# Output projection of a hybrid decoder layer: halves of 512 columns in four PSUM banks, where there were quarters of 256

## The chip, the cores and the metric

The kernel runs on one core of one Trainium2 chip. The metric is the device time of one execution in microseconds (us); the times before are the median of three runs and one profiled execution.

## The reference

The layer normalises 2048 positions of 1024 channels, projects them for three groups of heads, concatenates the groups' outputs (384 + 384 + 256 columns), maps them through one matrix and normalises the sum with the residual:

```python
hn = rmsnorm(x, norm_g)
a_in, a_gate, c_in, c_b, c_c, c_gate, q, q_gate = split(hn @ w_in)
y_ssm  = s5_group(a_in, ..., w_glu, b_glu) * silu(a_gate)      # 384 columns
y_conv = short_conv(c_in, c_b, c_c) * silu(c_gate)             # 384 columns
y_mem  = memory_cross_attention(q, rmsnorm(mem)) * silu(q_gate) # 256 columns
h = x + concat(y_ssm, y_conv, y_mem) @ w_out                   # w_out is 1024 x 1024
out = rmsnorm(h, final_norm_g)
```

The change is in the last two lines alone.

## The kernel before

The sequence is worked on in four quarters q = 0 to 3 of 512 positions. Every product of two float32 matrices is made of three matmuls on numbers that are split into a high and a low part (`mm3`: high by high at L81, high by low at L82, low by high at L83). `split` makes the parts: ScalarE (ACT) copies the high part (a CAST at L86), and then VectorE (DVE) or GpSimd (POOL) subtracts it for the low part (a TENSOR_TENSOR at L77). `wtile` loads a weight tile through SyncE's queue (SP) into a staging buffer and splits it.

The output projection of one quarter multiplies the 8 row tiles of y (three of the state-space group, `yssm`; three of the convolution, `yconv`; two of the attention, `ymem`; 128 rows each) by `w_out`. `outproj` goes over four quarters of 256 output columns (n_). For each it holds two PSUM banks, named po with the quarter, n_ and b: each bank holds two of the four blocks i of 128 positions, side by side. Two weight tiles of 512 rows by 256 columns (kh = 0 and 1) feed it, and for each tile and block `omm` issues 12 matmuls of 256 columns. One projection is 384 matmuls. VectorE then adds each bank to the residual h (`h<-po`, 128x512); that add is what returns the bank. After the last column, ScalarE squares and sums h (L101), a row of small operations on VectorE and GpSimd makes the scale, and four products of 1024 columns at L916 finish the rows.

The four projections run at four places of the program. In the code they are:

```python
    interleave(outproj(1), prep(2), 0.3, 2)     # L1019
    interleave(outproj(0), prep(3), 0.3, 2)     # L1022
    interleave(outproj(3), glu(2), 1.0)         # L1025
    outproj_last(2)                             # L1026
```

I call them projections one to four in this order. `interleave` puts steps of a second task between the steps of the projection: `prep` loads x for the next quarter (`xq`), normalises it (a chain of small operations q22v, q22r, q22a, q22o and a product at L602) and transposes it through TensorE (`trq`, L144) into `hn`; `glu` multiplies the state-space output by `w_glu` (tiles `wg`, banks `psg`, 27 matmuls of 512 columns) and makes the gate products `gt` and `ua`, whose split is `yssm`. `outproj_last` keeps all eight weight tiles in buffers that are free by then (`wyc`, `wym`, `wtb`, `hy` and so on) and finishes blocks 0 and 1 first, then block 2, then block 3.

A scheduler fixes the order of instructions on each engine before the kernel is run, and each engine runs its queue in order: an instruction that waits holds back all that stand behind it on its engine. PSUM has eight banks: three for all projections (`ps_mm`), two for transposes, one for the attention's output (`ps_po`), two for the state-space group (`ps_ss`; `psg` is there). Split weight tiles have three buffers, their staging two.

Of the kernel before, what the change touches and what calls it, by code (L numbers as in the profile page):

```python
# [28 lines left out]
QL = SEQ // NQ  # L29
# [16 lines left out]
def hymba_layer_kernel(  # L46
# [7 lines left out]
    V, S, G, T = nc.vector, nc.scalar, nc.gpsimd, nc.tensor  # L54
# [5 lines left out]
    kvp = ctx.enter_context(tc.tile_pool(name="kvp", bufs=1))  # L60
# [39 lines left out]
    def sumsq(xt, ss, junk):  # L100
        S.activation(junk, xt, AF.Square, accum_out=ss)  # L101
# [7 lines left out]
    fg_b = const.tile([P, DM], F32, name="fg_b")  # L109
# [513 lines left out]
    yv, Y = {}, {}  # L623
# [81 lines left out]
    vd = kvp.tile([P, 2, 2, HEADS, P], F32R, tag="vd", name="vd")  # L705
# [136 lines left out]
        yield  # L842


    yk = [("ssm", 0), ("ssm", 1), ("ssm", 2), ("conv", 0), ("conv", 1), ("mem", 0), ("mem", 1), ("conv", 2)]
    rows = [0, 1, 2, 3, 4, 6, 7, 5]

    def fetch_y(q):

# [13 lines left out]
                t = Y[q]["conv" if z + k < 3 else "mem"][:, :, (z + k) % 3]  # L863
                split(t[:, 0], t[:, 1], st[:, k], V if k else G)

    def omm(q, ps, i, kh, w, first):

        o_ = slice(i * P, (i + 1) * P)
        for k in range(4):
            nm, kk = yk[4 * kh + k]  # L870
            kr = rows[4 * kh + k] - 4 * kh
            mm3(ps, Y[q][nm][:, 0, kk, o_], Y[q][nm][:, 1, kk, o_], w[:, 0, kr, :], w[:, 1, kr, :],
                first and k == 0, kh == 1 and k == 3, skip_group_check=True)

    def residual(q, last=False):

# [9 lines left out]
                nc.sync.dma_start(h[z][u * NCH:(u + 1) * NCH], xq[q, u][:, 2 * z:2 * z + 2])  # L886
        return h

    def wout(q, n_, kh, dst=None, st="w", e=G):
        src = w_out[0, kh * 512:(kh + 1) * 512, n_ * 256:(n_ + 1) * 256]  # L890
        return wtile(src, 512, 256, f"wo{q}{n_}{kh}", e, dst, st)

    def outproj(q):
        h = residual(q)
        for n_ in range(4):
            ns = slice(n_ * 256, (n_ + 1) * 256)
            pss = [ps_mm.tile([P, 2, 256], F32, tag="mm", name=f"po{q}{n_}{b}") for b in range(2)]
            for kh in range(2):
                w = wout(q, n_, kh)
                for i in range(4):  # L900
                    omm(q, pss[i // 2][:, i % 2, :], i, kh, w, kh == 0 and i % 2 == 0)
                    yield
            for b in range(2):
                hb = h[b][:, :, ns]
                tt(hb, pss[b], hb, ALU.add)
        jk = tmp.tile([P, QL], F32, tag="ci", name=f"junk{q}")
        ss = sml.tile([P, 2, 4], F32, tag="ssf", name=f"ssf{q}")
        for i in range(4):
            for z in range(2):
                sumsq(h[i // 2][:, i % 2, z * QL:(z + 1) * QL], ss[:, z, i:i + 1], jk)  # L910
        tt(ss[:, 0], ss[:, 0], ss[:, 1], ALU.add)
        ss = ss[:, 0]
        r = row_rstd(ss, 4, "rf", f"f{q}")
        for i in range(4):
            hi_ = h[i // 2][:, i % 2]
            V.scalar_tensor_tensor(hi_, hi_, r[:, i:i + 1], fg_b, ALU.mult, ALU.mult)  # L916
            for u in range(2):
                nc.sync.dma_start(oq[q, u, :, i], hi_[u * NCH:(u + 1) * NCH])
        yield

    def outproj_last(q):

        h, hb = residual(q, True)
        for u in range(2):
            nc.sync.dma_start(hb[u * NCH:(u + 1) * NCH], xq[q, u][:, 2:4])
        hg = late["big"].tile([P, 2, DM], F32, tag="big1", name="hg")

        def wv_(t):
            return t[:, :2 * 4 * 256].rearrange("p (z k n) -> p z k n", z=2, k=4)

        dsts = [None, None, None, Y[q]["rest"].rearrange("p z a (b n) -> p z (a b) n", b=2)]
        dsts.append(wv_(kvp.tile([P, 2 * 4 * 256], F32R, tag="vd", name="wvd")))
        dsts.append(wv_(stab.tile([P, GB * TW], F32, tag="tb", name="wtb").bitcast(F32R)))
        dsts.append(wv_(late["yc"].tile([P, 2 * 3 * QL], F32R, tag="yc", name="wyc")))
        dsts.append(wv_(late["ym"].tile([P, 2 * 2 * QL], F32R, tag="ym", name="wym")))
        ws = [[wout(q, n_, kh, dsts[2 * n_ + kh], "wx"[kh], V if kh else G) for kh in range(2)] for n_ in range(4)]
        ss, jk = (sml.tile([P, 4, 4], F32, tag=t_, bufs=1, name=t_) for t_ in ("ssl", "ssk"))

        def rstd(i, nss):
            V.tensor_reduce(jk[:, i, 0:1], ss[:, i, 0:nss], AX.X, ALU.add)  # L940
            return row_rstd(jk[:, i, 0:1], 1, f"rl{i}", f"fl{i}")

        def store(i, src):
            for u in range(2):
                nc.sync.dma_start(oq[q, u, :, i], src[u * NCH:(u + 1) * NCH])

        junk = [tmp.tile([P, QL], F32, tag=t_, name="junk" + t_) for t_ in ("ci", "u")]
        for n_ in range(4):
            ns = slice(n_ * 256, (n_ + 1) * 256)
            ps = ps_mm.tile([P, 2, 256], F32, tag="mm", name=f"po{q}{n_}")  # L950
            for kh in range(2):
                for i in range(2):
                    omm(q, ps[:, i, :], i, kh, ws[n_][kh], kh == 0 and i == 0)
            for i in range(2):
                tt(h[i][:, ns], ps[:, i], h[i][:, ns], ALU.add)
                sumsq(h[i][:, ns], ss[:, i, n_:n_ + 1], junk[0][:, 0:256])
        for i in range(2):
            V.scalar_tensor_tensor(h[i], h[i], rstd(i, 4), fg_b, ALU.mult, ALU.mult)
            store(i, h[i])
        for i in range(2, 4):  # L960
            parts = [(0, 1), (2, 3)] if i == 2 else [(0, 1), (2,), (3,)]
            for b, ns_ in enumerate(parts):
                ns = slice(ns_[0] * 256, ns_[-1] * 256 + 256)
                ps = ps_mm.tile([P, 2, 256], F32, tag="mm", name=f"po{q}{i}_{b}")
                for a, n_ in enumerate(ns_):
                    for kh in range(2):
                        omm(q, ps[:, a, :], i, kh, ws[n_][kh], kh == 0 and a == 0)
                pv = ps.rearrange("p a n -> p (a n)")[:, :256 * len(ns_)]
                tt(h[i][:, ns], pv, h[i][:, ns], ALU.add)
                sumsq(h[i][:, ns], ss[:, i, b:b + 1], junk[1][:, :256 * len(ns_)])  # L970
                tt(hg[:, i - 2, ns], h[i][:, ns], fg_b[:, ns], ALU.mult)
            r = rstd(i, len(parts))
            V.tensor_scalar(h[i][:, :QL], hg[:, i - 2, :QL], r, None, ALU.mult)
            S.activation(h[i][:, QL:], hg[:, i - 2, QL:], AF.Copy, scale=r)  # L974
            store(i, h[i])
# [48 lines left out]
    fetch_y(2)  # L1024
    interleave(outproj(3), glu(2), 1.0)  # L1025
    outproj_last(2)  # L1026


# [27 lines left out]
```

## Time and profile before

| what | value |
| --- | --- |
| median of 3 runs | 902.94 us (900.92 to 909.04) |
| profiled execution | 904.45 us |
| its span (first to last instruction) | 902.5 us |
| mean granted clock of TensorE in the span | 0.975 |
| TensorE (PE) busy | 843.1 us, 93% |
| VectorE (DVE) busy | 613.7 us, 68% |
| ScalarE (ACT) busy | 367.0 us, 41% |
| GpSimd (POOL) busy | 301.7 us, 33% |

A row of a timeline gives the start of an instruction in us, its length, engine, line, operation, the tiles it writes and reads, its shape and how many such follow each other; in brackets stands how long the engine was idle just before it and what released it. Matmuls overlap, so that the pace of a run of them is the distance between starts, not the length of one. "Clock" is the share of TensorE's full clock that was granted: 1.00 is 2.4 GHz and 0.50 is 1.2 GHz.

### The profile page before, as it was taken

The numbers are of one execution on the slowest core, as the hardware profiler recorded it, in microseconds if no ns is written. First come the engines' busy times: TensorE is split into PE (matmuls) and PEld (weight loads), VectorE is DVE, ScalarE is ACT, GpSimd is POOL, SyncE is SP. The second block draws the span as 40 slices with busy tenths as digits, with TensorE's granted clock in tenths as the row PEclk, the third lists the DMA queues.
The fourth block names the chain that finished last, engine by engine and source line by source line (L and its number), as shares of the span: only waits on it lengthen the run. The fifth ranks groups of instructions, "written<-read, shape, count | busy, mean of one in ns | idle before, by whom it ended". The sixth has DMA issues, their size and how long they took to land. (4 is left out here: it accounts for less than half of the span.)

```text
span 902.5 us, 13173 instructions
## 1 busy us (share of the span) xinstructions
PE 843.1 (93%) x4876; PEld 723.7 (80%) x4876; DVE 613.7 (68%) x1244; ACT 367.0 (41%) x706; POOL 301.7 (33%) x157
## 2 busy tenths in 40 slices
PE   2998999889998998999999899999999998989996
PEld 2985777778877877899888688899878876879996
DVE  6898899583998896936434664344399996865353
ACT  5343433545343434433444533335233344444511
POOL 2000001154222344444545434334443343455400
PEclk9999899999997999999999999999999999999999
DMA  9553649966464534454575632656757744493362
GB/s 205 161 150 103 189 131 269 267 187 201 125 179 130 156 93 119 108 152 141 159 239 150 160 114 84 161 165 186 214 156 207 211 128 125 117 222 112 125 177 57
DMA packets 180647, 142.97 MB, mean 158 GB/s; under 512 B 41192, under 2 KB 164584, under 8 KB 180584
## 3 DMA queue, kind: packets, MB, share of 16 engines
q1 hardware_dynamic: 180584, 142.14, 56.4%
q8 instruction: 38, 0.62, 0.3%
q14 instruction: 25, 0.20, 0.1%
HBM read 113.80 MB, written 26.74 MB: 156 GB/s over the span
## 5 line engine op out<-in xcount | busy, mean ns | idle before, releaser
L77 POOL TENSOR_TENSOR wo<-wo_st,wo 128x1024 fp32r<-128x1024 f32 x26 | 63.8, 2454 | 70.6 <-ACT wo L86 59.2
L77 DVE TENSOR_TENSOR h<-po,h 128x512 f32<-128x512 f32 (+1 forms) x37 | 22.2, 615 | 43.5 <-PE po L83 34.5
L81 PE MATMUL po<-wo,yssm 128*128 128x256 f32 x168 | 48.5, 289 | 1.8 <-ACT yssm L86 1.8
L83 PE MATMUL po<-wo,yssm 128*128 128x256 f32 x168 | 48.2, 287 | 0.0
L82 PE MATMUL po<-wo,yssm 128*128 128x256 f32 x168 | 47.8, 285 | 0.0
L780 ACT ACTIVATE pe<-sps,nm 128x256 f32<-128x256 f32 x64 | 29.5, 472 | 39.4 <-DVE nm L778 35.1
L81 PE MATMUL psai<-hn,wai 128*128 128x512 f32 (+1 forms) x120 | 42.7, 362 | 2.8 <-ACT hn L86 2.1
L82 PE MATMUL psai<-hn,wai 128*128 128x512 f32 (+1 forms) x120 | 42.5, 356 | 0.3 <-DVE hn L77 0.2
L83 PE MATMUL psai<-hn,wai 128*128 128x512 f32 (+1 forms) x120 | 42.0, 353 | 0.0
L81 PE MATMUL pscg<-hn,wcg 128*128 128x512 f32 x96 | 39.8, 415 | 2.2 <-ACT wcg L86 2.2
L86 ACT CAST wo<-wo_st 128x1024 fp32r<-128x1024 f32 x27 | 28.2, 1044 | 33.3 <-PE po L83 16.2
L81 PE MATMUL po<-wo,yconv 128*128 128x256 f32 x144 | 40.7, 283 | 0.0
L83 PE MATMUL po<-wo,yconv 128*128 128x256 f32 x144 | 40.3, 280 | 0.0
L82 PE MATMUL po<-wo,yconv 128*128 128x256 f32 x144 | 40.1, 279 | 0.0
L83 PE MATMUL pscg<-hn,wcg 128*128 128x512 f32 x96 | 39.1, 407 | 0.5 <-DVE wcg L77 0.5
L81 PE MATMUL psag<-hn,wag 128*128 128x512 f32 x96 | 39.5, 411 | 0.0
L82 PE MATMUL pscg<-hn,wcg 128*128 128x512 f32 x96 | 39.0, 407 | 0.0
L77 POOL TENSOR_TENSOR wcb<-wcb_st,wcb 128x1024 fp32r<-128x1024 f32 x9 | 22.9, 2550 | 47.9 <-ACT wcb L86 47.9
L83 PE MATMUL psag<-hn,wag 128*128 128x512 f32 x96 | 38.5, 401 | 0.0
L82 PE MATMUL psag<-hn,wag 128*128 128x512 f32 x96 | 38.4, 400 | 0.0
L81 PE MATMUL pscb<-hn,wcb 128*128 128x512 f32 x96 | 38.3, 399 | 0.0
L81 PE MATMUL psci<-hn,wci 128*128 128x512 f32 x96 | 38.3, 399 | 0.0
(710 smaller groups left out, 2903.5 us busy)
## 6 DMA issues: line engine op xcount, KB each, us to landing
wo_st<-in_w_out_dram SPq DMA_DIRECT2D x32, 512.0 KB, 3.8
tb<-t_dram SPq DMA_DIRECT2D x16, 960.0 KB, 5.5
out_dram<-h SPq DMA_DIRECT2D x32, 256.0 KB, 3.4
h<-in_x_dram SPq DMA_DIRECT2D x14, 512.0 KB, 7.4
wai_st<-in_w_in_dram SPq DMA_DIRECT2D x12, 512.0 KB, 4.3
wag_st<-in_w_in_dram SPq DMA_DIRECT2D x12, 512.0 KB, 4.3
wci_st<-in_w_in_dram SPq DMA_DIRECT2D x12, 512.0 KB, 4.2
wcc_st<-in_w_in_dram SPq DMA_DIRECT2D x12, 512.0 KB, 4.1
```

Of the source, the lines that this page charges most:

```text
L77: e.tensor_tensor(o, a, b, op)
L81: T.matmul(ps, lh, rh, start=first, stop=False, **kw)
L82: T.matmul(ps, lh, rl, start=False, stop=False, **kw)
L83: T.matmul(ps, ll, rh, start=False, stop=last, **kw)
L86: S.copy(hi, src)
L780: S.activation(pe[:, a, h], sps[h][:, a], AF.Exp, bias=nm_[:, a, h:h + 1], accum_out=sm[:, a, h:h + 1])
```

## The change

The projection goes over two halves of 512 columns. Each of the four blocks i has a bank of its own: three banks of `ps_mm` and the one of `ps_po`. A weight tile is now 256 rows by 512 columns, that is two row tiles of y (a pair kp), and holds as many elements as before; the pairs are taken in the order 0, 1, 3, 2. A call of `omm` issues 6 matmuls of 512 columns. The list `yk` has the row tiles in plain order, so the table `rows` goes. `outproj_last` does the same for its blocks 0 and 1, takes block 2 in two parts of 512 columns and block 3 in parts of 512, 256 and 256; the sums of squares of blocks 0 and 1 have two pieces in place of four.

```diff
-    yk = [("ssm", 0), ("ssm", 1), ("ssm", 2), ("conv", 0), ("conv", 1), ("mem", 0), ("mem", 1), ("conv", 2)]
-    rows = [0, 1, 2, 3, 4, 6, 7, 5]
+    yk = [("ssm", 0), ("ssm", 1), ("ssm", 2), ("conv", 0), ("conv", 1), ("conv", 2), ("mem", 0), ("mem", 1)]
+    pairs = (0, 1, 3, 2)
...
-        for k in range(4):
-            nm, kk = yk[4 * kh + k]
-            kr = rows[4 * kh + k] - 4 * kh
-            mm3(ps, Y[q][nm][:, 0, kk, o_], Y[q][nm][:, 1, kk, o_], w[:, 0, kr, :], w[:, 1, kr, :],
-                first and k == 0, kh == 1 and k == 3, skip_group_check=True)
+        for k in range(2):
+            nm, kk = yk[2 * kp + k]
+            mm3(ps, Y[q][nm][:, 0, kk, o_], Y[q][nm][:, 1, kk, o_], w[:, 0, k, cs], w[:, 1, k, cs],
+                kp == pairs[0] and k == 0, kp == pairs[-1] and k == 1)
...
-        src = w_out[0, kh * 512:(kh + 1) * 512, n_ * 256:(n_ + 1) * 256]
+        src = w_out[0, kp * 256:(kp + 1) * 256, nh * 512:(nh + 1) * 512]
...
-        for n_ in range(4):
-            ns = slice(n_ * 256, (n_ + 1) * 256)
-            pss = [ps_mm.tile([P, 2, 256], F32, tag="mm", name=f"po{q}{n_}{b}") for b in range(2)]
-            for kh in range(2):
-                w = wout(q, n_, kh)
+        for nh in range(2):
+            ns = slice(nh * 512, (nh + 1) * 512)
+            pss = [ps_mm.tile([P, 512], F32, tag="mm", name=f"po{q}{nh}{b}") for b in range(3)]
+            pss.append(ps_po.tile([P, QL], F32, tag="po", name=f"po{q}{nh}3"))
+            for kp in pairs:
+                w = wout(q, nh, kp)
                 for i in range(4):
-                    omm(q, pss[i // 2][:, i % 2, :], i, kh, w, kh == 0 and i % 2 == 0)
+                    omm(q, pss[i], i, kp, w)
                     yield
-            for b in range(2):
-                hb = h[b][:, :, ns]
-                tt(hb, pss[b], hb, ALU.add)
+            for i in range(4):
+                hb = h[i // 2][:, i % 2, ns]
+                tt(hb, pss[i], hb, ALU.add)
...
-        for n_ in range(4):
-            ns = slice(n_ * 256, (n_ + 1) * 256)
-            ps = ps_mm.tile([P, 2, 256], F32, tag="mm", name=f"po{q}{n_}")
-            for kh in range(2):
+        for nh in range(2):
+            ns = slice(nh * 512, (nh + 1) * 512)
+            pss = [ps_mm.tile([P, 512], F32, tag="mm", name=f"po{q}{nh}{i}") for i in range(2)]
+            for kp in pairs:
                 for i in range(2):
-                    omm(q, ps[:, i, :], i, kh, ws[n_][kh], kh == 0 and i == 0)
+                    omm(q, pss[i], i, kp, ws[nh][kp])
```

The four projections have 1536 matmuls of 256 columns before; with the change they have 744 of 512 and 48 of 256. Everything outside the projections keeps its order, except a few neighbouring loads on SyncE's queue. Three places move within the engines' queues; names end in a running number.

TensorE at the start of projection one, before: banks po100 and po101 on the first weight tile wo100, then the transposes of `prep`; `yssm1` in the rows after the transposes is the third row tile of the state-space group, `yssm1` ahead of them the first two.

```order
L81 MATMUL po101_3667<-wo100_3670,yssm1_3351 128x256
L82 MATMUL po101_3667<-wo100_3670,yssm1_3351 128x256
L83 MATMUL po101_3667<-wo100_3670,yssm1_3351 128x256
L144 MATMUL trq20_0_3770<-ident_99,xq20_3751 128x128 x4
L144 MATMUL trq20_1_3822<-ident_99,xq20_3751 128x128
L81 MATMUL po100_3666<-wo100_3670,yssm1_3351 128x256
L82 MATMUL po100_3666<-wo100_3670,yssm1_3351 128x256
```

The same place with the change, where the third row tile comes with the second weight tile, wo101:

```order
L83 MATMUL po101_3667<-wo100_3672,yssm1_3351 128x512
L81 MATMUL po103_3669<-wo100_3672,yssm1_3351 128x512
L82 MATMUL po103_3669<-wo100_3672,yssm1_3351 128x512
L83 MATMUL po103_3669<-wo100_3672,yssm1_3351 128x512
L81 MATMUL po100_3666<-wo101_3701,yssm1_3351 128x512
L82 MATMUL po100_3666<-wo101_3701,yssm1_3351 128x512
L81 MATMUL po101_3667<-wo101_3701,yssm1_3351 128x512
L83 MATMUL po100_3666<-wo101_3701,yssm1_3351 128x512
```

Ahead of the first matmul on the third row tile there stood 12 matmuls of 256 columns and 5 transposes; now 18 of 512 columns stand there, and the transposes come later.

TensorE in projection three, around the first matmul of `glu` (bank psg20, weight tile wg20), before:

```order
L83 MATMUL po301_7331<-wo301_7426,ymem3_6906 128x256
L81 MATMUL po310_7527<-wo310_7531,yssm3_6918 128x256
L81 MATMUL po300_7330<-wo301_7426,ymem3_6906 128x256
L82 MATMUL po300_7330<-wo301_7426,ymem3_6906 128x256
L81 MATMUL po301_7331<-wo301_7426,ymem3_6906 128x256
L82 MATMUL po301_7331<-wo301_7426,ymem3_6906 128x256
L81 MATMUL psg20_7408<-yssm2_7349,wg20_7405 128x512
L82 MATMUL psg20_7408<-yssm2_7349,wg20_7405 128x512
```

And with the change:

```order
L81 MATMUL po303_6949<-wo301_7020,yssm3_6534 128x512
L82 MATMUL po303_6949<-wo301_7020,yssm3_6534 128x512
L83 MATMUL po303_6949<-wo301_7020,yssm3_6534 128x512
L81 MATMUL psg20_7002<-yssm2_6961,wg20_6999 128x512
L82 MATMUL psg20_7002<-yssm2_6961,wg20_6999 128x512
L81 MATMUL po303_6949<-wo301_7020,yconv3_6122 128x512
L82 MATMUL po303_6949<-wo301_7020,yconv3_6122 128x512
L83 MATMUL psg20_7002<-yssm2_6961,wg20_6999 128x512
```

Ahead of the first psg20 matmul stood 65 matmuls of 256 columns of the projection; now 45 of 512 stand there.

VectorE in projection one, where `prep` normalises its third block (q22, xq22) and TensorE goes from the first columns to the next, before:

```order
L77 TENSOR_TENSOR q22a_4006<-q22r_4005 128x1
L77 TENSOR_TENSOR q22a_4006<-q22a_4006,q22v_4004 128x1
L96 TENSOR_SCALAR q22a_4006<-q22a_4006 128x1
L77 TENSOR_TENSOR q22o_4007<-q22r_4005,q22a_4006 128x1
L602 SCALAR_TENSOR_TENSOR xq22_3996<-xq22_3996,q22o_4007,ng_b_106 128x1024
L77 TENSOR_TENSOR hn2_3750<-trq21_0_3901,hn2_3750 128x4x128
L77 TENSOR_TENSOR h10_3660<-po110_3803,h10_3660 128x2x256
L77 TENSOR_TENSOR h11_3661<-po111_3804,h11_3661 128x2x256
```

And with the change, where these are the adds at the end of the first half, which return the four banks to the second half:

```order
L77 TENSOR_TENSOR q22a_3894<-q22r_3893 128x1
L77 TENSOR_TENSOR h10_3660<-po100_3666,h10_3660 128x512
L77 TENSOR_TENSOR q22a_3894<-q22a_3894,q22v_3892 128x1
L96 TENSOR_SCALAR q22a_3894<-q22a_3894 128x1
L77 TENSOR_TENSOR q22o_3895<-q22r_3893,q22a_3894 128x1
L77 TENSOR_TENSOR hn2_3716<-trq21_0_3821,hn2_3716 128x4x128
L602 SCALAR_TENSOR_TENSOR xq22_3884<-xq22_3884,q22o_3895,ng_b_106 128x1024
L77 TENSOR_TENSOR h10_3660<-po101_3667,h10_3660 128x512
L77 TENSOR_TENSOR h11_3661<-po102_3668,h11_3661 128x512
L77 TENSOR_TENSOR h11_3661<-po103_3669,h11_3661 128x512
```

The add of the first bank stands inside the chain, the adds of the other three behind the product at L602. In projection four the adds of the first half (po200, po201) stand on VectorE behind the four products of L916, where the add of the first bank of 256 columns stood ahead of them.

## Rows read from the trace of the kernel before

**Rows 1.** The page: busy time, share of the span, instructions; granted clock in 40 slices.
```profile
PE 843.1 (93%) x4876; PEld 723.7 (80%) x4876; DVE 613.7 (68%) x1244; ACT 367.0 (41%) x706; POOL 301.7 (33%) x157
PEclk9999899999997999999999999999999999999999
```

**Rows 2.** Windows, one per projection: us, PE busy (count), clock, DMA share, GB/s.
```profile
381.01:433.26 52.25, 50.43 (x417) 0.97 0.54 146
578.25:626.52 48.27, 48.27 (x417) 1.00 0.69 196
791.31:848.37 57.06, 53.07 (x412) 0.97 0.64 171
848.37:893.84 45.47, 45.47 (x386) 1.00 0.42 117
```

**Rows 3.** Timeline of PE: first matmuls that bound runs without a wait.
```profile
433.26 0.40 PE L81 MATMUL psai<-hn,wai 128*128 128x512 f32 x1
...
449.61 0.39 PE L81 MATMUL psq<-hn,wq 128*128 128x512 f32 x1
...
826.13 0.28 PE L81 MATMUL po<-wo,yssm 128*128 128x256 f32 x1
```

**Rows 4.** Windows of PE after waits and, fourth row, in a run.
```profile
386.56:389.97 3.41, 3.41 (x18) 0.50 0.83 174
389.97:393.38 3.41, 3.41 (x31) 1.00 0.46 153
802.50:806.49 3.99, 3.90 (x10) 0.57 1.04 186
788.53:791.31 2.78, 2.78 (x13) 1.00 0.43 109
...
354.20:362.00 7.80, 6.18 (x28) 1.00 0.48 135
675.40:679.00 3.60, 1.71 (x12) 1.00 0.50 148
```

**Rows 5.** Timelines of PE, ACT and DVE at the start of projection one.
```profile
384.96 0.39 PE L81 MATMUL po<-wo,yssm 128*128 128x256 f32 x1 [1.81 <-ACT yssm L86]
...
384.29 0.62 ACT L86 CAST yssm<-ua 128x512 fp32r<-128x512 f32 x1 [0.76 <-DVE ua L838]
...
384.94 0.94 DVE L77 TENSOR_TENSOR yssm<-ua,yssm 128x512 fp32r<-128x512 f32 x1 [0.74 <-ACT yssm L86]
```

**Rows 6.** Timelines of PE, ACT and DVE in projection three, around `glu`'s tiles.
```profile
802.49 0.50 PE L81 MATMUL psg<-yssm,wg 128*128 128x512 f32 x1 [3.40 <-ACT wg L86]
...
810.64 0.50 PE L81 MATMUL psg<-yssm,wg 128*128 128x512 f32 x1 [0.50 <-ACT wg L86]
...
801.92 0.51 ACT L86 CAST wg<-wg_st 128x384 fp32r<-128x384 f32 x1 [4.44 <-DMA wg_st<-in_w_glu_dram]
...
810.08 0.51 ACT L86 CAST wg<-wg_st 128x384 fp32r<-128x384 f32 x1 [2.64 <-DMA wg_st<-in_w_glu_dram]
...
802.47 0.88 DVE L77 TENSOR_TENSOR wg<-wg_st,wg 128x384 fp32r<-128x384 f32 x1 [0.67 <-ACT wg L86]
```

**Rows 7.** Timelines in the middle of projection one: VectorE, GpSimd, SyncE.
```profile
406.06 2.40 DVE L77 TENSOR_TENSOR q22a<-q22r 128x1 f32<-128x1 f32 x1 [0.66 <-POOL q22r L77]
...
409.06 1.28 DVE L602 SCALAR_TENSOR_TENSOR xq<-xq,q22o,ng_b 128x1024 f32<-128x1024 f32 x1
...
410.86 1.28 DVE L77 TENSOR_TENSOR h<-po,h 128x512 f32<-128x512 f32 x2
...
406.03 2.41 POOL L77 TENSOR_TENSOR wo<-wo_st,wo 128x1024 fp32r<-128x1024 f32 x1
...
398.70 1.14 SPq L572 DMA_DIRECT2D xq<-in_x_dram  x2
```

**Rows 8.** Timeline of VectorE in projection four.
```profile
859.46 4.87 DVE L916 SCALAR_TENSOR_TENSOR h<-h,f3o,fg_b 128x1024 f32<-128x1024 f32 x4
864.25 0.75 DVE L77 TENSOR_TENSOR h<-po,h 128x256 f32<-128x256 f32 x2
```

More of the change, by code (lines that the diff above doesn't have):

```diff
@@ L864, in fetch_y, with omm @@
                 split(t[:, 0], t[:, 1], st[:, k], V if k else G)
-    def omm(q, ps, i, kh, w, first):
+    def omm(q, ps, i, kp, w, cs=slice(0, 512)):
         o_ = slice(i * P, (i + 1) * P)
-        for k in range(4):
-            nm, kk = yk[4 * kh + k]
-            kr = rows[4 * kh + k] - 4 * kh
-            mm3(ps, Y[q][nm][:, 0, kk, o_], Y[q][nm][:, 1, kk, o_], w[:, 0, kr, :], w[:, 1, kr, :],
-                first and k == 0, kh == 1 and k == 3, skip_group_check=True)
+        for k in range(2):
+            nm, kk = yk[2 * kp + k]
+            mm3(ps, Y[q][nm][:, 0, kk, o_], Y[q][nm][:, 1, kk, o_], w[:, 0, k, cs], w[:, 1, k, cs],
+                kp == pairs[0] and k == 0, kp == pairs[-1] and k == 1)
     def residual(q, last=False):
@@ L887, in residual, with wout @@
         return h
-    def wout(q, n_, kh, dst=None, st="w", e=G):
-        src = w_out[0, kh * 512:(kh + 1) * 512, n_ * 256:(n_ + 1) * 256]
-        return wtile(src, 512, 256, f"wo{q}{n_}{kh}", e, dst, st)
+    def wout(q, nh, kp, dst=None, st="w", e=G):
+        src = w_out[0, kp * 256:(kp + 1) * 256, nh * 512:(nh + 1) * 512]
+        return wtile(src, 256, 512, f"wo{q}{nh}{kp}", e, dst, st)
     def outproj(q):
         h = residual(q)
-        for n_ in range(4):
-            ns = slice(n_ * 256, (n_ + 1) * 256)
-            pss = [ps_mm.tile([P, 2, 256], F32, tag="mm", name=f"po{q}{n_}{b}") for b in range(2)]
-            for kh in range(2):
-                w = wout(q, n_, kh)
+        for nh in range(2):
[4 more added lines that the diff above has]
+                w = wout(q, nh, kp)
                 for i in range(4):
-                    omm(q, pss[i // 2][:, i % 2, :], i, kh, w, kh == 0 and i % 2 == 0)
+                    omm(q, pss[i], i, kp, w)
                     yield
-            for b in range(2):
-                hb = h[b][:, :, ns]
-                tt(hb, pss[b], hb, ALU.add)
+            for i in range(4):
+                hb = h[i // 2][:, i % 2, ns]
+                tt(hb, pss[i], hb, ALU.add)
         jk = tmp.tile([P, QL], F32, tag="ci", name=f"junk{q}")
@@ L928, in wv_ @@
         def wv_(t):
-            return t[:, :2 * 4 * 256].rearrange("p (z k n) -> p z k n", z=2, k=4)
-        dsts = [None, None, None, Y[q]["rest"].rearrange("p z a (b n) -> p z (a b) n", b=2)]
-        dsts.append(wv_(kvp.tile([P, 2 * 4 * 256], F32R, tag="vd", name="wvd")))
+            return t[:, :2 * 2 * 512].rearrange("p (z k n) -> p z k n", z=2, k=2)
+        dsts = [None, None, None, Y[q]["rest"]]
+        dsts.append(wv_(kvp.tile([P, 2 * 2 * 512], F32R, tag="vd", name="wvd")))
         dsts.append(wv_(stab.tile([P, GB * TW], F32, tag="tb", name="wtb").bitcast(F32R)))
@@ L935, in outproj_last @@
         dsts.append(wv_(late["ym"].tile([P, 2 * 2 * QL], F32R, tag="ym", name="wym")))
-        ws = [[wout(q, n_, kh, dsts[2 * n_ + kh], "wx"[kh], V if kh else G) for kh in range(2)] for n_ in range(4)]
+        ws = [{kp: wout(q, nh, kp, dsts[4 * nh + a], "wx"[a % 2], V if a % 2 else G) for a, kp in enumerate(pairs)}
+              for nh in range(2)]
         ss, jk = (sml.tile([P, 4, 4], F32, tag=t_, bufs=1, name=t_) for t_ in ("ssl", "ssk"))
@@ L954, in outproj_last @@
             for i in range(2):
-                tt(h[i][:, ns], ps[:, i], h[i][:, ns], ALU.add)
-                sumsq(h[i][:, ns], ss[:, i, n_:n_ + 1], junk[0][:, 0:256])
+                tt(h[i][:, ns], pss[i], h[i][:, ns], ALU.add)
+                sumsq(h[i][:, ns], ss[:, i, nh:nh + 1], junk[0])
         for i in range(2):
-            V.scalar_tensor_tensor(h[i], h[i], rstd(i, 4), fg_b, ALU.mult, ALU.mult)
+            V.scalar_tensor_tensor(h[i], h[i], rstd(i, 2), fg_b, ALU.mult, ALU.mult)
@@ L959, in outproj_last @@
             store(i, h[i])
         for i in range(2, 4):
[L961 to L970, printed above, removed]
+            parts = [(0, 512), (512, 1024)] if i == 2 else [(0, 512), (512, 768), (768, 1024)]
@@ L971, in outproj_last @@
+            for b, (c0, c1) in enumerate(parts):
+                ns = slice(c0, c1)
+                ps = ps_mm.tile([P, 512], F32, tag="mm", name=f"po{q}{i}_{b}")[:, :c1 - c0]
+                for kp in pairs:
+                    omm(q, ps, i, kp, ws[c0 // 512][kp], slice(c0 % 512, c0 % 512 + c1 - c0))
+                tt(h[i][:, ns], ps, h[i][:, ns], ALU.add)
+                sumsq(h[i][:, ns], ss[:, i, b:b + 1], junk[1][:, :c1 - c0])
                 tt(hg[:, i - 2, ns], h[i][:, ns], fg_b[:, ns], ALU.mult)
```

## The prediction

> **What bounds the kernel now.** I read the page's busy shares first. TensorE is busy 93% of the span, VectorE 68%, and nearly all slices have TensorE at full clock [rows 1]: so what counts is the number and pace of matmuls, and the few places where TensorE waits. Then I cut the span into the four projections, the only stages that the change touches [rows 2]. Projections one and two have the same instructions, 384 matmuls of 256 columns and 32 transposes, but one takes 52.25 us and two 48.27; two has no idle time, one has. Three is 57.06 us with 4.0 idle; four has none. Together they are 203 us. Last I read the waits inside them in the timelines. Wherever the waits are gone, TensorE itself is the bound, and only a faster pace helps.
>
> **The pace.** 72 matmuls of 512 columns run from 433.26 to 449.61 without a wait: 227.1 ns each. The second half of projection three, from 826.13 to 848.37, is 192 matmuls of 256 columns and nothing else: 115.8 ns each, 231.7 for a pair [rows 2, 3]. A pair that becomes one matmul saves 4.6 ns, times 192 pairs a projection, 0.88 us; for projections one to three 2.6 us. Projection four takes 45.47 us for 384, 236.8 ns a pair [rows 2]; at 227.1 each of its 168 pairs saves 9.7 ns, 1.6 us (24 pairs stay as they are). Together -4.3 us. The other bound: the 12 matmuls of 512 columns just ahead of projection three took 2.78 us, 231.7 ns each [rows 4]; at that pace projections one to three gain nothing and four gains 168 x 5.1 ns, 0.9 us. I take 227.1, since it is a run of 72 in a row with the same operand types, and keep -0.9 for the range.
>
> The Trainium skill, "TensorE: Matmul & The Clock Gate", section "Back-to-back issue gap", gives the isolated gap of a matmul at full clock as its columns by 2.4 plus 2.5 ns: 109.2 for 256 columns, 215.8 for 512. By that a pair would save 2.5 ns, 1.9 us over 744 pairs in place of 4.3, and the whole sum would come to 893.6. The trace disagrees on both sizes: 115.8 and 227.1.
>
> **The wait at the start of projection one.** TensorE idles 1.81 us until ScalarE's CAST of the third `yssm` row tile, and then runs at half clock from 386.56 to 389.97: 18 instructions there, 31 in the next 3.41 us [rows 4, 5]. Against projection two the whole costs 52.25 - 48.27 = 4.0 us: 1.8 waiting, 3.41 x 0.5 = 1.7 of clock, 0.5 of small gaps. With the change 18 matmuls of 512 columns stand ahead of the third tile, so TensorE comes there at 381.01 + 18 x 0.2271 = 385.10. The high part is done at 384.29 + 0.62 = 384.91, the low part at 384.94 + 0.94 = 385.88; the first matmul that needs the low one comes three later, at 385.78 [rows 5]. A wait of 0.1 is left: -3.9 us. What comes next is weight tile wo101, split before the projection begins. If the 0.1 grows and the clock falls anyway, 1.7 of the 3.9 stays.
>
> **The waits in projection three.** Its first half, 791.31 to 826.13, takes 34.82 us; 192 matmuls at 115.8 ns are 22.24 and 27 of `glu` at 227.1 are 6.13, so 6.4 us are lost [rows 2, 3]: waits of 3.40 and 0.50 for `wg` tiles [rows 6], 3.99 x 0.43 = 1.7 us of clock behind the first [rows 4], and 0.8 of small gaps. With the change 45 matmuls of 512 columns (in place of 65 of 256) stand ahead of psg20: TensorE comes at 791.31 + 45 x 0.2271 = 801.53. The tile's load is not moved, and ScalarE's CAST ends at 801.92 + 0.51 = 802.43 [rows 6]. A wait of 0.9 is left. The low part, at 803.35 [rows 6], is wanted four matmuls later, at 803.34: nothing. psg21 has 81 matmuls ahead of it: 791.31 + 0.9 + 81 x 0.2271 = 810.6, its CAST ends at 810.59 [rows 6]: nothing. Does a wait of 0.9 bring the clock down? After 1.81 it fell; but two windows with 1.6 and 1.9 us of idle time in them kept 1.00 [rows 4], so I take that it stays up. -5.5 us; the bounds are -3.0 (1.7 of clock and 0.8 of gaps stay) and -6.4.
>
> **What the change adds: banks that come back in fours.** Before, a projection held two of three banks, and the next columns began in the third. Now all four are held; at the end of a half TensorE needs the first one back at once. Its add (0.64 us, [rows 7]) can run once the last pair is through with block 0, 18 matmuls or 4.1 us before the half ends. But in projections one and two it stands in VectorE's queue behind q22a, and the three other adds behind the product at L602. That chain starts with the load of xq22, which went out at 398.70, after the last transpose of xq20 [rows 7]. In the new order that transpose has 54 matmuls and 7 transposes of about 0.12 us ahead of it: 381.01 + 12.3 + 0.8 = 394.1, 4.5 us earlier. If the chain moves by that, q22a starts at 401.6 and the first add is done at 402.4 to 404.6; TensorE ends the half at 381.01 + 96 x 0.2271 + 16 x 0.12 = 404.7. L602 then ends at 405.8, and the three adds by 408.4, while the other banks are wanted from 407.2 on, some 1.4 us apart. So it just fits. But q22a, one column wide, took 2.40 us while GpSimd ran a subtraction of 2.41 us from 406.03 on [rows 7]; where they meet depends on the new times. Behind a late add in VectorE's queue stand the copies `hn<-trq`, which return transpose banks, and TensorE waits for those too. I charge 0.5 us in each of the two projections; bounds 0 and 2.4, the row of q22a. In projection three VectorE is nearly idle at the half's end: 0.
>
> In projection four po211 needs the bank of po200, whose add stands behind the four products of L916. These end at 859.46 + 4.87 = 864.33, 16.0 us after the projection's start, the add 0.7 later [rows 8]; TensorE comes there after 72 matmuls, 16.35 us. Its wait is 0.35 if nothing ahead of the products is later than before; the sums of squares and GpSimd's step are. I charge 1.0; bounds 0 and 3.4 (the longest wait in these rows [rows 6]).
>
> Loads and splits have the same number, size and staging as before, and each weight tile feeds 24 matmuls of 512 columns in place of 48 of 256, so nothing there. The two sums of squares fewer a block run on ScalarE, beside TensorE. The end after the last matmul is unchanged.
>
> **The sum.** -4.3 - 3.9 - 5.5 + 1.0 + 1.0 = -11.7 us. From the profiled 904.45 that gives 892.75; the median of the runs lies 1.5 lower, so 902.94 - 11.7 = 891.2 us.
>
> **The rivals.** First, the clock still falls behind the shorter waits in projections one and three: 1.7 of the one and 2.5 of the other stay. For it: half clock follows both waits there now [rows 4]. Against: two idle times of that size that cost no clock [rows 4]. -11.7 + 4.2 = -7.5, 895.4 us; if projection four waits its 3.4 as well, 897.8.
>
> Second, the change doesn't give the pace that it is made for: 512 columns at 231.7 ns. -0.9 for -4.3 gives -8.3, 894.6 us. For it: one such run [rows 4]. Against: the run of 72.
>
> Third, the other side: the banks come back late at each boundary. If xq22's chain is not earlier than before, the first add of projection one ends at 406.06 + 2.40 + 0.64 = 409.1, while TensorE wants the bank at 404.7: 4.4 us, and half clock behind it another 1.7, 6.1 in place of the 0.5 charged, in projections one and two; in projection four 3.4 + 1.7 = 5.1 in place of 1.0. That is +15.3 on -11.7: 906.5 us, slower than before. It decides from (11.7 + 2.0) / 3 = 4.6 us a boundary on, clock included. Against it: the load of xq22 waits for a transpose that does come earlier. The Trainium skill has a rule for this: the same page, section "A second HAM failure mode: psum-queue depth-cycling", tells of a kernel with matmuls of 512 columns that cycled through PSUM banks, idled shortly between groups and lost its clock over and over. The trace of before doesn't show it: there the next columns always found a spare bank.
>
> Fourth, better: nothing of the added waits comes, and projection three loses all its 6.4: -14.6, 888.3 us.
>
> **How the numbers follow.** Forecast 0.53, clock 0.22, pace 0.12, late banks 0.08, better 0.05. The forecast's own spread, with 0 to 2.4 twice and 0 to 3.4 for the costs, is 888 to 896. The range of 885 to 901 takes in all cases but the third, and half of what lies between it and the first. 1% is 9.0 us, about what a measurement of this kernel can tell from no change; it puts the border at 893.9. Below it lie most of the forecast (0.46), the better case (0.05) and a part of the two middle ones (0.06): 0.57 faster. Slower by over 1% would be 912, which needs the third case and a wait in projection three as well: 0.04. The rest, 0.39, is the same.
>
> **What would show it.** Right: starts of matmuls 227 ns apart in the projections; projections one and two 47 to 48 us, three 50 to 51, four 45; no wait over 0.5 us for `yssm` at 385 and one near 0.9 before psg20; adds of the first bank done before the second half's first matmul. Wrong: slices of TensorE at half clock at the middles of the projections, with `h<-po` as what ended the wait; pairs at 232 ns; a load of xq22 that goes out no earlier.

## The result, and the profile after

The changed kernel takes 896.89 us (median of 8 runs, 895.24 to 899.31) where the kernel before took 903.98 (8 runs beside them): a ratio of 0.9921, 95% interval 0.9898 to 0.9944. That is 7.1 us less, by 0.8%: the whole interval lies below 1, but the gain is within the 1% that the prediction calls the same; 11.7 us had been forecast. The page of its profile, busy time and granted clock [rows 1]:

```profile
span 895.1 us, 11674 instructions
PE 837.5 (94%) x4132; PEld 686.3 (77%) x4132; DVE 613.9 (69%) x1240; ACT 365.1 (41%) x698; POOL 300.7 (34%) x157
PEclk9999899989997999999999999999999999999998
```

The windows of its four projections [rows 2], then one behind the wait at psg20 [rows 4], then the last 96 matmuls of projection three (stretch, us, PE busy with count, clock, DMA share, GB/s):

```profile
382.10:431.43 49.33, 48.39 (x226) 1.00 0.56 152
575.57:623.70 48.13, 48.05 (x226) 1.00 0.68 198
786.46:840.83 54.37, 52.15 (x221) 0.97 0.63 178
840.83:886.44 45.61, 44.28 (x217) 1.00 0.43 119
800.49:803.90 3.41, 3.41 (x9) 0.50 1.06 304
818.91:840.83 21.92, 21.92 (x98) 1.00 0.52 162
```

Projection one is 2.9 us shorter, two 0.1 and three 2.7, and four is 0.1 longer: 5.6 us less in all. The rest of the span's 7.4 lies in stretches that the change doesn't touch: 1.1 us more ahead of projection one, 0.8 less between one and two, 2.0 less between two and three. The wait at the start of one is gone, with its half clock. Four waits of TensorE are left, here from its timeline with what ended them:

```profile
407.26 0.47 PE L81 MATMUL po<-wo,yssm 128*128 128x512 f32 x1 [0.92 <-DVE q22a L77]
797.87 0.50 PE L81 MATMUL psg<-yssm,wg 128*128 128x512 f32 x1 [1.02 <-ACT wg L86]
800.27 0.64 PE L83 MATMUL psg<-yssm,wg 128*128 128x512 f32 x1 [1.21 <-DVE wg L77]
858.73 0.50 PE L81 MATMUL po<-wvd,yssm 128*128 128x512 f32 x1 [1.33 <-DVE h L77]
```

And VectorE at these places: the chain of q22 with the first bank's add [rows 7], the weight tile of the gate behind the subtraction for `yconv` [rows 6], and the add of po200 behind the four products [rows 8]:

```profile
404.14 2.38 DVE L77 TENSOR_TENSOR q22a<-q22r 128x1 f32<-128x1 f32 x1 [0.66 <-POOL q22r L77]
406.44 0.68 DVE L77 TENSOR_TENSOR h<-po,h 128x512 f32<-128x512 f32 x1
...
795.81 2.86 DVE L77 TENSOR_TENSOR yconv<-uc,yconv 128x512 fp32r<-128x512 f32 x1
798.60 1.62 DVE L77 TENSOR_TENSOR wg<-wg_st,wg 128x384 fp32r<-128x384 f32 x1
...
853.20 4.88 DVE L916 SCALAR_TENSOR_TENSOR h<-h,f3o,fg_b 128x1024 f32<-128x1024 f32 x4
857.99 0.68 DVE L77 TENSOR_TENSOR h<-po,h 128x512 f32<-128x512 f32 x1
```

Each of the four waits ends with VectorE or, for the high part, with ScalarE's CAST: at these places, 4.5 of the 197.4 us, the path has gone from TensorE's own pace to what the other two give back. (The profile puts the first wait down to the small q22a behind the add; e_ss below shows that it is the bank's.)

My theory after this one execution: the gain is the pace, the start of one and a part of three; what is missing is that three keeps two waits and one piece of half clock, and that the banks cost 0.9 and 1.3 us. The rivals: that the pace brought less than all this, or nothing; and that the missing part is chance in stretches elsewhere.

### The profile page after: what moved, and what is told of

Read it like the earlier page. It is cut to its first block, busy times and chain, and to the rows that moved or that the text cites. A ratio compares the mean times of both kernels' runs of the same rounds, so it can differ in the third digit from the quotient of the medians.

```text
span 895.1 us, 11674 instructions
## 1 busy us (share of the span) xinstructions
PE 837.5 (94%) x4132; PEld 686.3 (77%) x4132; DVE 613.9 (69%) x1240; ACT 365.1 (41%) x698; POOL 300.7 (34%) x157
## 5 line engine op out<-in xcount | busy, mean ns | idle before, releaser
L81 PE MATMUL psai<-hn,wai 128*128 128x512 f32 (+1 forms) x120 | 43.4, 368 | 3.8 <-ACT hn L86 2.8
L82 PE MATMUL psai<-hn,wai 128*128 128x512 f32 (+1 forms) x120 | 43.2, 362 | 0.3 <-DVE hn L77 0.2
L83 PE MATMUL psai<-hn,wai 128*128 128x512 f32 (+1 forms) x120 | 42.7, 359 | 0.0
L81 PE MATMUL pscb<-hn,wcb 128*128 128x512 f32 x96 | 38.3, 399 | 0.0
L81 PE MATMUL psci<-hn,wci 128*128 128x512 f32 x96 | 38.2, 398 | 0.0
L81 PE MATMUL pscc<-hn,wcc 128*128 128x512 f32 x96 | 38.2, 398 | 0.0
L83 PE MATMUL pscb<-hn,wcb 128*128 128x512 f32 x96 | 37.7, 393 | 0.0
L82 PE MATMUL pscc<-hn,wcc 128*128 128x512 f32 x96 | 37.7, 392 | 0.0
L83 PE MATMUL psci<-hn,wci 128*128 128x512 f32 x96 | 37.7, 392 | 0.0
L82 PE MATMUL pscb<-hn,wcb 128*128 128x512 f32 x96 | 37.6, 392 | 0.0
L83 PE MATMUL pscc<-hn,wcc 128*128 128x512 f32 x96 | 37.6, 392 | 0.0
L82 PE MATMUL psci<-hn,wci 128*128 128x512 f32 x96 | 37.6, 392 | 0.0
```

## The experiments

All ratios are to the kernel before, run beside them on the same chip. It took 905.1 to 906.0 us there, so that the changed kernel, at 0.9921, stands for 897.9 to 898.9, 1 to 2 us above the 896.9 that the expectations start from. The lengths in us of the projections, and of the stretch from the end of two to the start of three, are from one profiled execution each:

| run | one | two | two to three | three | four | ratio (95%) |
| --- | --- | --- | --- | --- | --- | --- |
| before | 52.25 | 48.27 | 164.79 | 57.06 | 45.47 | |
| changed | 49.33 | 48.13 | 162.77 | 54.37 | 45.61 | 0.9921 (0.9898 to 0.9944) |
| again | 49.68 | 48.06 | 164.99 | 53.31 | 46.47 | 0.9928 (0.9901 to 0.9954) |
| e256 | 51.99 | 50.09 | 163.25 | 55.67 | 48.19 | 1.0029 (1.0013 to 1.0045) |
| e_ss | 48.18 | 47.53 | 163.48 | 54.44 | 45.65 | 0.9902 (0.9874 to 0.9930) |
| e_bank | 49.27 | 48.05 | 164.94 | 52.78 | 44.49 | 0.9900 (0.9857 to 0.9943) |
| e_wg | 48.94 | 48.07 | 164.05 | 56.57 | 44.03 | 0.9899 (0.9860 to 0.9937) |
| a_late | 49.21 | 48.10 | 165.78 | 52.00 | 45.39 | 0.9910 (0.9890 to 0.9929) |
| e_late | 47.97 | 47.54 | 163.43 | 53.25 | 44.00 | 0.9890 (0.9858 to 0.9922) |
| b_shift | 51.79 | 49.67 | 164.90 | 56.51 | 45.23 | 0.9993 (0.9971 to 1.0015) |
| a_shift | 49.30 | 48.10 | 165.04 | 53.08 | 46.48 | 0.9916 (0.9888 to 0.9943) |
| e_best | 48.28 | 47.73 | 165.70 | 54.50 | 43.94 | 0.9910 (0.9878 to 0.9942) |

**The pace by itself (pace).** The starts of matmuls in both traces fell into clusters (113 and 120 ns for 256 columns, 227 and 233 for 512), so I measured trains with nothing beside them.

```python
for width in (512, 256):
    for so in range(2):          # stationary operand: 0 or 64 bytes behind a multiple of 128
        for mo in range(2):      # moving operand: the same
            train(f"r{r}w{width}s{so}m{mo}", so, mo, width, 8)
```

> This kernel leaves the whole layer out and runs trains of matmuls alone, 96 of 512 columns or 192 of 256 in each, twice, with the stationary and the moving operand beginning at a multiple of 128 bytes (0) or 64 bytes behind one (1). Theory A: the pace depends on whether the two begin alike. Alike (0-0 and 1-1): 226.7 ns for 512 columns and 120 for 256, so that a pair of 256 becomes 13 ns cheaper as one. Unlike (0-1, 1-0): 229 to 233 for 512 and 113 to 115 for 256, so that a pair becomes dearer by up to 6 ns or stays. Theory B: columns alone set it; all four cases lie within 1 ns, at 227 and 116.

Windows of the eight trains of the first round: stationary and moving at 0-0, 0-1, 1-0, 1-1, first 96 matmuls of 512 columns, then 192 of 256:

```profile
73.89:95.65 21.76, 21.76 (x98) 1.00 0.00 1
95.65:118.05 22.40, 22.40 (x98) 1.00 0.00 1
118.05:140.45 22.40, 22.40 (x98) 1.00 0.00 0
140.45:162.25 21.80, 21.80 (x98) 1.00 0.00 1
162.25:185.27 23.02, 23.02 (x193) 1.00 0.01 1
185.27:207.05 21.78, 21.78 (x194) 1.00 0.00 1
207.05:228.82 21.77, 21.77 (x195) 1.00 0.01 2
228.82:251.85 23.03, 23.03 (x195) 1.00 0.00 1
```

Theory A holds and B falls. Where the operands begin alike, 512 columns take 226.7 ns and 256 take 119.9; where they don't, 233.3 and 113.4. A pair of 256 is 13 ns dearer than one of 512 in the first case and 6.5 cheaper in the second. The Trainium skill's formula for an isolated matmul ("TensorE: Matmul & The Clock Gate", "Back-to-back issue gap": columns by 2.4 plus 2.5 ns) gives 2.5 ns for a pair in every case; no train shows that.

**The same structure with 256 columns (e256).**

```diff
-            mm3(ps, ..., w[:, 0, k, cs], w[:, 1, k, cs], ...)
+            for c in range(cs.start, cs.stop, 256):
+                mm3(ps[:, c - cs.start:c - cs.start + 256], ..., w[:, 0, k, c:c + 256], w[:, 1, k, c:c + 256], ...)
```

> The changed kernel, with each matmul of 512 columns of the projections issued as two of 256, all else in the same order: undoes the pace alone. Theory A (operands that begin alike gain 13 ns a pair, the others nothing): projections one, two and three are 0.7 us longer each, less what their waits give back, four 1.2 us, in all 2.5 to 3.3 over the changed kernel's 896.9, about 900. Theory B (4.6 to 9.7 ns on every pair): 4.3 us longer, 901.2. Theory C (512 columns gain nothing): 896.9.

It took 908.42 us, 1.0029: some 9.5 us above the changed kernel, and slower than the kernel before. No theory had that much. The expectation's "all else in the same order" was wrong, since the scheduler plans anew for the other durations; projections one and two alone have waits of 1.54, 1.09 and 1.08 us for VectorE that the changed kernel doesn't have, like this one:

```profile
412.32 0.39 PE L81 MATMUL po<-wo,yssm 128*128 128x256 f32 x1 [1.09 <-DVE h L77]
```

So this run can't be read as the price of the pace. It does show that four banks and halves without the wide matmuls, in the order that they then get, are a small loss: what the change gains hangs on the 512 columns and the order that goes with them, and this run can't tell the two apart.

**The pace in place (b_shift and a_shift).** Both have word for word the order of the kernel that they come from; only the place of one tile differs.

```diff
-        ty = stab.tile([P, 3 * 2 * QL], F32, tag="tb", name=f"yssm{q}")
-        y_ssm = ty.bitcast(F32R).rearrange("p (z t n) -> p z t n", z=2, t=3)
+        ty = stab.tile([P, 3 * 2 * QL + 32], F32, tag="tb", name=f"yssm{q}")
+        y_ssm = ty.bitcast(F32R)[:, 16:16 + 3 * 2 * QL].rearrange("p (z t n) -> p z t n", z=2, t=3)
```

> The kernel before, with the state-space tile yssm beginning 64 bytes later, so that 540 of the 1536 matmuls of 256 columns have operands that begin unlike where they began alike, and 36 the other way; the order of all instructions is the same. Theory A (113.4 ns unlike, 120 alike): 504 x 6.6 ns = 3.3 us faster in the matmuls, projection two 48.27 to 47.3 us, the whole 0.3 to 0.4% under the kernel before. Theory B (the pace is of columns alone, and what differs in the trains is the trains' own): no change.

> The changed kernel with the same shift of yssm; the order is the same. Theory A (512 columns: 227 alike, 229 to 233 unlike): the other sign, 270 matmuls 2 to 6 ns slower, 0.5 to 1.6 us longer, projection two 48.1 to 48.3 to 48.6 us. Theory B (columns alone): no change. A third theory, that the shift itself relieves some engine, would make both kernels faster.

Neither time moved: 0.9993 (0.9971 to 1.0015) to before, and 0.9916 against the changed kernel's 0.9921. Projection one of b_shift is 0.46 us shorter and three 0.55, as A says in kind, but two is 1.4 longer, with one wait of 0.66 us in it and all its matmuls nearer 118 ns, the ones not moved too. The four projections together are 0.15 us longer, where A had worked out 3.3 shorter, so A's price is not shown, and something else that I did not find sets the pace when other engines run. The rule of the trains stands for trains alone.

**The banks (e_ss and e_bank).**

```diff
-            pss = [ps_mm.tile([P, 512], F32, tag="mm", name=f"po{q}{nh}{b}") for b in range(3)]
+            two = nh == 1 and q < 2
+            pss = [(ps_ss if two and b < 2 else ps_mm).tile([P, 512], F32, tag="ss" if two and b < 2 else "mm",
+                                                            name=f"po{q}{nh}{b}") for b in range(3)]
```

> The changed kernel, with the first two blocks of the second half of projections one and two in the two banks that the state-space group leaves idle there, so that the half begins with no bank back. Theory A (the add behind q22a costs the 0.92 us at 406): projection one 49.3 to 48.4 us, two unchanged at 48.1, the whole 896.0. Theory B (VectorE is late anyway, and TensorE then waits for the transposes' banks or the third block's): projection one stays at 49.0 to 49.4.

```diff
-            pss = [ps_mm.tile([P, 512], F32, tag="mm", name=f"po{q}{nh}{i}") for i in range(2)]
+            pss = [(ps_po if nh * i else ps_mm).tile([P, 512], F32, tag="po" if nh * i else "mm", name=f"po{q}{nh}{i}")
+                   for i in range(2)]
```

> The changed kernel, with po211 of the last projection in the attention's bank, so that it needs no bank back. Theory A (the bank behind the four products on VectorE costs the 1.33 us in the trace): projection four 45.6 to 44.3 us, the whole 895.6. Theory B (the weight tiles behind it are no earlier, so the wait moves to wtb, wyc or to the end): projection four stays at 45.4 to 45.6, the whole at 896.9.

Projections one and two of e_ss, then four of e_bank:

```profile
382.52:430.70 48.18, 48.07 (x226) 1.00 0.57 156
575.87:623.40 47.53, 47.53 (x225) 1.00 0.69 201
```

```profile
838.06:882.55 44.49, 44.41 (x216) 1.00 0.44 127
```

Theory A holds in both, but for two, which it had unchanged: busy and elapsed time nearly agree, and against the first execution one is 1.15 us shorter, two 0.6 (more than the timeline's waits had shown), four 1.12. That is what the banks cost there. It is no fixed price: e_wg below, without the edit of po211, has 44.03 us in four and no wait for that bank; its projection three is 2.2 us longer, and the add of po200 begins 15.6 us after the start of four in place of 17.2. The whole kernels' times, 0.9902 and 0.9900, lie below the changed kernel's 0.9921 by about that, but the intervals overlap.

**The waits in projection three (e_wg, a_late, again).** First the tiles earlier:

```diff
+        pre = []
+        for m in range(3 if q == 2 else 0):
+            pl, tg, nb = (swk, "ain", 2) if m else (tmp, "ue", 1)
+            pre.append(pl.tile([P, 3, P], F32, tag=tg, bufs=nb, name=f"wg{q}{m}_st"))
+            nc.sync.dma_start(pre[m], ...)
```

> The changed kernel, with the three weight tiles of the last gate step loaded as soon as their places are free, the first into a buffer that is idle by then (the scheduler then puts psg20 after 12 and psg21 after 54 matmuls of the projection). Theory A (projection three keeps two waits of 1.0 and 1.2 us for the first tile and 1.7 us of half clock behind them; without them it is the pace alone): projection three 54.4 to 50.7 to 51.5 us, no half clock, the whole 3 us under the changed kernel. Theory B (the wait moves to psg21, whose low part stands behind the long subtraction for yconv on VectorE): projection three stays above 53 us.

The timeline of its TensorE, and a window behind it:

```profile
799.38 0.50 PE L81 MATMUL psg<-yssm,wg 128*128 128x512 f32 x1 [1.57 <-ACT wg L86]
...
802.41 0.80 PE L83 MATMUL psg<-yssm,wg 128*128 128x512 f32 x1 [2.07 <-DVE wg L77]
```

```profile
800.55:807.38 6.83, 4.97 (x12) 0.50 1.04 306
```

Theory B: these are psg21's matmuls. The load of its tile landed at 798.7, its low part stands behind the subtractions on VectorE, and the half clock is twice as long. Projection three is 56.57 us, worse than before the edit. An earlier load alone only moves the wait, since the scheduler pulls the matmuls ahead with it. The whole kernel is no longer for it, at 0.9899; three and four together are 100.6 us where they were 99.98. So I moved the matmuls back in place of the loads forward:

```diff
-    interleave(outproj(3), glu(2), 1.0)
+    interleave(outproj(3), glu(2), 1.0, 8)
```

> The changed kernel with the steps of the gate task started 8 steps later in projection three; the scheduler then puts all but one of psg20's matmuls after 73 matmuls of the projection (16.6 us) in place of 45 to 49, when the low part of the weight tile is ready (13.8 us). Theory A (the waits of 1.0 and 1.2 us and the half clock in three are the part of the forecast gain that did not come): projection three 54.4 to 51 to 52 us, no half clock in it, the whole 2.5 to 3.5 us under the changed kernel. Theory B (what is gained there is given back at the end of three or in four, where the gate step's output or the residual's adds are late): three and four together stay at 99 to 100 us.

> The changed kernel once more, unchanged, beside the two below. Theory A (projection three and the stretch ahead of it share one loss of 1.7 us of half clock, which falls in the one or in the other): projections one, two and four within 0.3 us of 49.33, 48.13 and 45.60; the stretch between two and three plus projection three 217 to 218.2 us, as in the runs with other edits, wherever the half clock falls. Theory B (the half clock belongs to psg20's wait): again in projection three, 54.4 us, and none ahead of it.

Projection three of a_late; then, of the changed kernel run again, the stretch from two to three, projection three, and the half clock in the former:

```profile
788.78:840.78 52.00, 50.48 (x220) 1.00 0.65 178
```

```profile
623.12:788.11 164.99, 158.62 (x797) 0.99 0.57 161
788.11:841.42 53.31, 50.44 (x221) 1.00 0.65 177
...
762.21:765.62 3.41, 3.41 (x9) 0.50 0.91 255
```

The wait at psg20 in that second execution, the low part of its tile, and a wait for a bank at the end of three:

```profile
799.32 0.50 PE L81 MATMUL psg<-yssm,wg 128*128 128x512 f32 x1 [0.82 <-ACT wg L86]
...
799.30 0.88 DVE L77 TENSOR_TENSOR wg<-wg_st,wg 128x384 fp32r<-128x384 f32 x1 [0.67 <-ACT wg L86]
...
841.42 0.47 PE L81 MATMUL po<-wo,yssm 128*128 128x512 f32 x1 [2.06 <-DVE h L77]
```

In the second execution the same program had no half clock in three (0.8 us of wait at psg20 in place of 1.0 and 1.2), but one ahead of it, behind the wait of an earlier gate step. Theory B of that run falls: the half clock doesn't come with psg20's wait each time. Stretch and projection together are 218.30 us there, 0.1 over what A allowed, and 217.14 in the first execution, against 221.85 before; the other runs with unchanged work there, e_ss, e_bank and a_shift, have 217.7 to 218.1. Projections one (0.35) and four (0.86 over) were outside what A allowed: the banks' waits are 1.20 and 1.71 us in that execution.

These five executions fall into two kinds. In again, e_bank and a_shift the half clock came ahead of three, as in the kernel before; the low part of psg20's tile was done 12.1 to 12.3 us after the start of three (12.0 before), nothing in three ran at half clock, and the end of three holds a wait for a bank of 2.06, 1.28 and 1.21 us, which is part of the lengths in the table. In the first execution and in e_ss no half clock came ahead of three; the low part was done at 13.8 us, half clock fell in three, and its end holds no such wait. So the two kinds lose about the same by different ways.

a_late has projection three at 52.0, no half clock in it and no wait at psg20, and three and four together at 97.4 us against 99.98 and 99.78, as theory A has it. But it can't show that the half clock in three is removed: its execution has one ahead of three, as again has, where three has none either. Against again three is 1.3 us shorter and four 1.1: the waits of 0.82 and 2.06 us in three are gone, that in four is 1.09 in place of 1.71, and a new one for a bank has come at the middle of three:

```profile
820.80 0.51 PE L81 MATMUL po<-wo,yssm 128*128 128x512 f32 x1 [1.52 <-DVE h L77]
```

With the stretch ahead of three counted in, a_late has 263.2 us to the end of four, the changed kernel 262.7 and 264.8. The whole was 897.39 against 898.68 beside it, half of what A had, with overlapping intervals.

**All together (e_best, e_late).** e_best takes the banks, the early loads and this shift of `yconv` and `ymem`, after which all wide matmuls of the projections have operands that begin alike:

```diff
+    def at64(tag, n_, name, view=...):
+        return view(late[tag].tile([P, 2 * n_ * QL + 32], F32R, tag=tag, name=name)[:, 16:16 + 2 * n_ * QL])
```

> The changed kernel with all that helped or should: po211 in its own bank, the second halves of projections one and two in idle banks, the early loads for the last gate step, and yconv and ymem moved by 64 bytes so that all operands of 512 columns begin alike. Theory A (the parts add: 1.1 + 1.7 + 3 + 1.2): 7 us under the changed kernel, near 890. Theory B (the waits removed come back at the next bank or tile): 893 or more.

It took 898.78 us, 0.9910: theory B. The projections are 3.0 us shorter than the changed kernel's, less than half of the sum: the early loads put 2.2 us of wait and a half clock back into three, and the shift of `yconv` and `ymem` shows no gain, since one and two are 48.28 and 47.73 us where e_ss, without it, has 48.18 and 47.53.

> The same later gate task, with the idle banks for the second halves of projections one and two and the attention's bank for po211: projections 48.2, 47.5, 51 to 52 and 44.5 us, in all 5 to 6 us under the changed kernel, near 0.986 of the kernel before. Rival: the add of po201 and the banks at the start of four bring 1 to 2 us back, 0.988.

e_late, with the banks and the later gate steps, took 895.89 us, 0.9890 (0.9858 to 0.9922), the fastest of all medians, 2.8 us under the changed kernel beside it (the intervals overlap). The rival was right in kind: one, two and four are as expected, but three is 53.25, with a wait of 1.69 us for a bank at its middle, which the later gate steps brought, as in a_late; nothing was late at the start of four:

```profile
814.28 0.50 PE L81 MATMUL po<-wo,yssm 128*128 128x512 f32 x1 [1.69 <-DVE h L77]
```

This execution is of the first one's kind, with no half clock ahead of three and the low part of psg20's tile done 14.0 us after its start. The first 19.88 us of projection three, here and in the first execution of the changed kernel:

```profile
781.12:801.00 19.88, 19.53 (x86) 1.00 0.96 230
```

```profile
786.46:806.34 19.88, 17.66 (x70) 0.91 0.95 241
```

With the later gate steps 86 matmuls of the same width run where 70 ran, and none at half clock: the 16 are 3.6 us at 227 ns each, near the two waits and the lost clock (2.2 and 1.7 us) less the 0.35 that e_late waits for the first of them. That shows what these cost in three. The wait of 1.69 us for a bank took back about half of it.

## Why the prediction was right, and where it was not

Direction and mechanism held, the size was 0.6 of what was said, and in the windows of the projections alone, 5.6 us, half of it; the range of 885 to 901 held the time. The gain fell in the class within 1%, to which 0.39 was given and not the 0.57. Nearly all terms missed on the same side, so no errors cancelled. Point by point, measured in the first execution:

- **The pace**, forecast -4.3. The last 192 matmuls of projection three took 22.24 us [rows 2, 3], the 96 in their place 21.92: 3.3 ns a pair, where 4.6 was used. Projection four without its wait of 1.33 is 44.28 against 45.47: -1.2, where -1.6 was used. With 3 x 0.64 that makes -3.1. The run at 227.1 is nearly all of one kind: 67 of its 72 starts lie 226 or 227 ns apart, the pace of the trains with operands that begin alike. The 192 were a mixture, 72 on `yssm` some 120 ns apart and 120 on `yconv` and `ymem` some 113 apart; with 512 columns the former came at 227 and the latter at 225 to 232. So the price of one kind was used for both.
- **The start of projection one**, forecast -3.9. No wait is left there. Without the bank waits (e_ss) one is 0.65 us longer than two, where it was 3.98 longer: -3.3.
- **Projection three**, forecast -5.5, the term that missed by most. "A wait of 0.9 is left": 1.0 was. For the low part, four matmuls later, it had nothing: 1.2 us. "I take that it stays up": half clock from 800.49 to 803.90, 1.7 us. Measured -2.7, and -2.05 without the pace. I had let the low part be done 12.0 us after the start of the projection, as before; it was done at 798.60 + 1.62 = 800.22, 13.8 after it. TensorE came to projection three 1.7 us earlier against VectorE than before: the stretch ahead of it was 2.0 us shorter, because its half clock did not fall this time, while VectorE's long subtractions went on as they do. I had held VectorE's times fixed to the projection's start, and nothing ties them to it. The second execution bears this out: the half clock did fall ahead of three, the low part was done at 799.30 + 0.88 = 800.18, 12.1 after the start, and the wait was 0.8 with no half clock behind it, as forecast. There the gain went elsewhere, to the 2.06 us for a bank at the end of three, for which the prediction has no term; without it three would be 51.25 us. Together with the stretch ahead, three is 4.7 and 3.6 us shorter in the two executions, against -6.4 forecast for three with its pace. e_late shows that in the first kind of execution the waits and the half clock were the cause within three.
- **The banks in projections one and two**, charged 0.5 each: 1.15 and 0.6. The chain of q22 did come earlier (q22a 22.0 us after the start, 25.1 before; I had 20.6), but q22a met GpSimd's subtraction again and took 2.38 us. The bound of 2.4 was the length of q22a, which came true at 2.38; some half of it, 1.15, became cost in one.
- **The bank of po200 in four**, charged 1.0: waits of 1.33 and 1.71, of which e_bank gave 1.12 back.
- **The sum**: -3.1 - 3.3 - 2.05 + 1.15 + 0.6 + 1.33 = -5.4, for 5.6 in the windows. The 1.8 us beyond it in the profiled pair I take for chance, which is argued and not shown: e_bank, e_ss and e_late have the same instructions ahead of projection one and reach it at 378.75, 382.52 and 377.97 us, and the 2.0 us between two and three came back in the second execution, where the windows of the projections give 5.5.

Of the rivals, the first (half clock behind shorter waits, 895.4) came nearest: it was so in three in the first execution, and not in one. The second holds in part (3.3 ns of the 4.6). The third was right on the mechanism and wrong on its price: the banks were late by 0.6 to 2.1 us a place and without half clock, where 4.6 was needed. Beside it stands the kernel of which the Trainium skill ("TensorE: Matmul & The Clock Gate", "A second HAM failure mode: psum-queue depth-cycling") tells that short idle times between its groups of matmuls took the clock down again and again. This trace does not agree: the clock in projections one, two and four is 1.00 with those waits in them.

What stays open: what sets the pace of unlike operands beside working engines, and on what it depends whether the wait of some 2.4 us ahead of projection three costs its half clock; it did with 2.44 us before and 2.37 in the second execution of the changed kernel, and did not with 2.35 in the first and 2.44 in e_late.

## What to carry to other kernels

When TensorE is sped up in one stage, the times at which other engines deliver don't move with it: count each of them from what releases it, not from the stage's start, and expect that a part of the gain turns into waits at the next things that VectorE hands over. A change that takes all banks of a pool at once needs its first bank back at once; a bank that is idle in that stage, found by looking at who uses each pool when, paid 0.6 to 1.15 us a place here. And a pace read from one row is worth no more than that row's operands; look at where they begin before using it for others.

## What the runs showed of the hardware that was not expected

In trains alone the pace of these matmuls depends on where the stationary and the moving operand begin: a multiple of 128 bytes apart, or 64 bytes more, the only two cases tried, gave 226.7 against 233.3 ns for 512 columns and 119.9 against 113.4 for 256, with the sign turned round between the two widths. In the whole kernel the rule was blurred, and moving one tile by 64 bytes changed no time that could be measured. A VectorE operation of one column took 2.38 us beside a subtraction of 2.40 us on GpSimd that began 0.04 us before it, where like ones with GpSimd idle take 0.16.
